# Expert layer of a two-block model: plain fp32 router, first expert pair picked by one-hot products, expert results read back by plain transfers

## The chip, the cores and the metric

The kernel runs on one core of one Trainium2 chip. The metric is the device time of one execution in microseconds, as the median of several runs; lower is better.

## The reference

Two transformer blocks on 512 tokens of 1024 features, all in fp32. The first block (sparse attention, convolution, feed-forward) and the first half of the second (a gated mixer) end in `x`. What the change touches is the second half of the second block, a mixture of 32 experts, and the last norm:

```python
h = modulate(rms_norm_2(x, norm2_g), shift2, scale2)          # (1 + scale2) * norm + shift2
x = x + gate2 * hierarchical_moe(h, ...)
return rms_norm_2(x, final_norm_g)

def hierarchical_moe(h, ...):                                  # 512 tokens, 4 groups of 8 experts
    grp = argmax(softmax(h @ w_group + b_group))               # one group for each token
    top_p, top_e = top_k(softmax((h @ w_router + b_router)[grp]), 2)
    weights = p_grp * top_p / sum(top_p)                       # two experts for each token
    # each token's row goes to its two experts, and the two weighted results are added
    y[token] += (silu(h @ w_gate[e]) * (h @ w_up[e])) @ w_down[e] * weight
```

## The kernel before, in words

The first block fills 0 to about 650 us and the mixer about 650 to 1140 us. From 1140 to 1232 us the output projection of the mixer runs (`join`), with the router beside it; after that the experts run to 1519 us and the last norm to the end.

**Router.** `route_tile` takes a tile of 128 tokens: eight transposes of `x` on PE (L215), their split into two halves of lower precision (ACT L200, DVE L201), the square sum on ACT (L1319) and the inverse root on POOL (`rsqrt`, L211). `rest` makes 24 matmuls with the weights stationary and a transpose back; `end` makes the logits `LT` (L1330), then the normed row `h` (tile `xg`): a multiplication on DVE (L1331) and two additions of 512 columns each (L1334), on POOL for the first three tiles and on DVE for the last. `h` is stored in DRAM (`h2d`, L1335). The four tiles of `h` also stay in the chip's memory as `xg0` to `xg3`.

**Routing.** `route` is a chain of small DVE operations and one-hot products on PE. It gives `tab`, the tokens of each job (`table`, products L1561), and `to`, the place of each result. After the first table, twelve matmuls whose result nobody reads (L1580, `warm`) are on PE. `rest` makes the tables of the other jobs.

**Jobs.** A job (`Pair`) is two experts of up to 64 tokens each; there are 17 (`NP`). The weights are 96 panels of 1 MB, two for each of gate, up and down, loaded by SP into 17 places in rotation (`place`, `panel_of`); a panel starts when the matmuls that read the panel before it in its place are done. Of a job: `gather` (an indirect load by POOL of 128 rows of `h2d`, L1915, into one of two buffers), `turn` (eight transposes, L215, and copies to `xT`, L1928), `up` (64 products of gate and up, L1937, into `a`), `turn_a`, and `down` (16 products, scaled by DVE L1972). Jobs 0 to 12 write rows into `ye` in DRAM (POOL, L1986). Jobs 13 to 16 are "hot" (`HOT` = 13): their rows go back to the tokens on PE, by products with a one-hot matrix `oh` (16 DVE operations, L2000; `spread`, products L2009, additions L2017; the last two jobs in `tail`).

**Results of jobs 0 to 12.** `results` (L1476, L1479) clears a place and gathers for each token the two rows of `ye` that are not hot; for tiles 0 and 1 during job 14, for tiles 2 and 3 during job 15. DVE adds the two rows to `x` one after the other (L1395). A second use of `results`, for experts with more tokens than two jobs hold, is skipped here.

The compiler's scheduler sets the order of the instructions on each engine; POOL's DMAs stand in POOL's order with its arithmetic, and SP's in SP's.

## Time and profile before

| | |
|---|---|
| median of 3 runs | 1540.04 us (1537.99 to 1541.09) |
| the profiled execution's own time | 1541.89 us |
| its span, first to last instruction | 1540.0 us |
| mean granted TensorE clock | 0.978 of full speed |
| PE / DVE / ACT / POOL busy | 95 / 57 / 37 / 13% |
| bytes moved | 266.97 MB, mean 173 GB/s |

The profile is of one execution, and its own time is 1.85 us above the median. Times in its rows count from the first instruction. PE is busy nearly everywhere, so the shares tell little; what counts here is which wait ends last in the stretch from 1224 us to the end.

### The profile page before, as it was taken

To read this page: it belongs to the slowest core of one execution; us is meant where nothing else is said; L and a number is where in the kernel's file an instruction comes from. 1 tells how busy PE (TensorE), PEld (TensorE's weight loads), DVE (VectorE), ACT (ScalarE), POOL (GpSimd) and SP (SyncE) were. 2 spreads that over 40 slices of the span, in tenths; PEclk is the share of its full clock that TensorE was granted. 3 is DMA by queue.
4 is the path that set the end of the run, shared out by engine and by line. 5 is a ranking of instruction groups with operands and counts; after the bars stand their busy time and mean duration, and the time that the engine had idled before them with its cause. 6 is when DMAs were issued, how large, how long until landed. Compare 5 with 4: busy or idle time off the path is not lost.

```text
span 1540.0 us, 20461 instructions
## 1 busy us (share of the span) xinstructions
PE 1460.1 (95%) x7678; PEld 1146.2 (74%) x7678; DVE 883.8 (57%) x1903; ACT 575.5 (37%) x1219; POOL 204.2 (13%) x233
## 2 busy tenths in 40 slices
PE   7999899999999999999999999999999969998885
PEld 6877678787888888887888888888887845555542
DVE  5665687967666764466785452327755763211162
ACT  4444575743242332334444442226643201110112
POOL 2110131100101010040000020000002411111400
PEclk8999999999999999999999999999999979999998
DMA  5225202038665654333322315331149479999971
GB/s 190 91 74 165 93 28 69 28 121 264 199 210 164 203 194 150 124 129 121 96 87 77 84 58 168 130 123 39 45 160 346 164 304 363 420 423 424 423 324 56
DMA packets 132768, 266.97 MB, mean 173 GB/s; under 512 B 19194, under 2 KB 78619, under 8 KB 120376
## 3 DMA queue, kind: packets, MB, share of 16 engines
q1 hardware_dynamic: 119834, 241.90, 43.9%
q0 software_dynamic: 9376, 20.89, 3.7%
q10 hardware_dynamic: 3454, 2.82, 0.6%
q8 instruction: 62, 1.02, 0.3%
q14 instruction: 42, 0.34, 0.1%
HBM read 253.66 MB, written 21.54 MB: 179 GB/s over the span
## 4 chain that ended last, share of the span: by engine, by line
PE 67%; DMA 13%; DVE 6%; ACT 2%; issue 1%; POOL 1%; SPq 0%; ACTq 0%; DVEq 0%; POOLq 0%
PE b L154 18%; PE b L155 18%; PE b L156 18%; PE b L1937 6%; DMA pw<-w_expert_gate 4%; DMA pw<-w_expert_down 3%; PE b L215 3%; DMA pw<-w_expert_up 3%; DMA gm<-gd 1%; DVE wl L148 1%; PE b L819 1%; DMA xg<-h2d,tab 1%; PE b L820 1%; PE b L762 1%; DMA wr<-w_up 1%
## 5 line engine op out<-in xcount | busy, mean ns | idle before, releaser
L148 DVE TENSOR_TENSOR wl<-wr,wh 128x512 fp32r<-128x512 f32 x349 | 237.1, 716 | 146.0 <-ACT wh L146 134.3
L146 ACT ACTIVATE wh<-wr 128x512 fp32r<-128x512 f32 x361 | 205.3, 622 | 301.5 <-PE b L155 142.3
L1937 PE MATMUL b<-pw,xT 128*64 128x256 f32 x1088 | 135.0, 395 | 7.5 <-DMA pw<-w_expert_up 7.1
L1937 PEld LDWEIGHTS b<-pw,xT 128*64 128x64 f32 x1088 | 85.1, 142 | 53.9 <-issue 10.8
L156 PE MATMUL b<-h2h,wl 128*128 128x512 f32 (+1 forms) x320 | 121.3, 379 | 0.0
L154 PE MATMUL b<-h2h,wh 128*128 128x512 f32 (+1 forms) x320 | 121.2, 380 | 0.0
L155 PE MATMUL b<-h2l,wh 128*128 128x512 f32 (+1 forms) x320 | 121.2, 379 | 0.0
L155 PE MATMUL b<-fl,wh 128*128 128x512 f32 (+1 forms) x288 | 105.2, 366 | 0.0
L154 PE MATMUL b<-fh,wh 128*128 128x512 f32 (+1 forms) x288 | 104.9, 366 | 0.3 <-ACT fh L200 0.3
L156 PE MATMUL b<-fh,wl 128*128 128x512 f32 (+1 forms) x288 | 105.1, 366 | 0.0
L155 PE MATMUL b<-wl,uh 128*128 128x512 f32 x256 | 99.9, 390 | 0.5 <-DVE wl L148 0.5
L154 PE MATMUL b<-wh,uh 128*128 128x512 f32 x256 | 100.2, 391 | 0.1
L156 PE MATMUL b<-wh,ul 128*128 128x512 f32 x256 | 99.8, 390 | 0.0
L495 DVE SCALAR_TENSOR_TENSOR acc<-wr,cond,acc 128x512 f32<-128x512 f32 x84 | 62.9, 749 | 38.2 <-DMA wr<-mod_w 36.4
L1954 DVE SCALAR_TENSOR_TENSOR a<-b,ws,a 128x256 f32<-128x256 f32 x17 | 8.2, 483 | 106.5 <-PE b L1937 106.5
L156 PEld LDWEIGHTS b<-h2h,wl 128*128 128x128 f32 x320 | 60.2, 188 | 11.3
L155 PEld LDWEIGHTS b<-h2l,wh 128*128 128x128 f32 x320 | 60.2, 188 | 11.1
L154 PEld LDWEIGHTS b<-h2h,wh 128*128 128x128 f32 x320 | 60.1, 188 | 10.9
L1937 PE MATMUL b<-pw,aT 128*64 128x512 f32 x272 | 64.9, 597 | 0.0
L154 PEld LDWEIGHTS b<-fh,wh 128*128 128x128 f32 x288 | 54.1, 189 | 9.5 <-ACT fh L200 0.5
L155 PEld LDWEIGHTS b<-fl,wh 128*128 128x128 f32 x288 | 54.3, 189 | 9.0 <-DVE fl L201 0.2
L156 PEld LDWEIGHTS b<-fh,wl 128*128 128x128 f32 x288 | 54.3, 189 | 8.8
(601 smaller groups left out, 3256.9 us busy)
## 6 DMA issues: line engine op xcount, KB each, us to landing
wr<-w_in SPq DMA_DIRECT2D x33, 1024.0 KB
pw<-w_expert_gate SPq DMA_DIRECT2D x32, 1024.0 KB
pw<-w_expert_up SPq DMA_DIRECT2D x32, 1024.0 KB
pw<-w_expert_down SPq DMA_DIRECT2D x32, 1024.0 KB
wr<-mod_w SPq DMA_DIRECT2D x24, 1024.0 KB
wr<-w_up SPq DMA_DIRECT2D x16, 1024.0 KB
wr<-w_down SPq DMA_DIRECT2D x16, 1024.0 KB
wr<-w_cmp SPq DMA_DIRECT2D x4, 1024.0 KB
```

The costliest lines, as they stand in the source:

```text
L146: nc.scalar.activation(hi[:, c], raw[:, c], AF.Copy)
L148: (nc.gpsimd if i in pool else eng or nc.vector).tensor_tensor(lo[:, c], raw[:, c], hi.bitcast(F32)[:, c], op=ALU.subtract)
L154: mm(o, lh, rh, start=first, stop=False)
L155: mm(o, lh, rl, start=False, stop=False)
L156: mm(o, ll, rh, start=False, stop=last)
L215: self.nc.tensor.transpose(o, i, self.ident[:k, :k])
L495: nc.vector.scalar_tensor_tensor(acc, rv[:, k, :], self.cond[:, kk:kk + 1], acc, op0=ALU.mult, op1=ALU.add)
L762: nc.tensor.matmul(b[:, :n], QS[:, h, qs], KH[:, kind, g, :n], start=True, stop=False)
L819: nc.tensor.matmul(o, v, ph, start=kind == 2, stop=False)
L820: nc.tensor.matmul(o, v, pl, start=False, stop=kind == 1 and kb == qb)
L1937: self.nc.tensor.matmul(o[h, :], x[:, k, h], w[s](k), start=k == ks[0], stop=k == ks[-1])
L1954: nc.vector.scalar_tensor_tensor(self.a, gu[1], em.ws[:, self.c:self.c + 1], self.a, op0=ALU.mult, op1=ALU.mult)
```

## The change

1. The load of `x` for the mixer of the first block is issued after the fourth step of a plan, in place of before it.
2. The router multiplies in plain fp32: the transposes are copied, one half by ACT and one by DVE, without a split; the tokens are stationary and the 36 columns of weights move, 8 matmuls for a tile in place of 24, and their result needs no transpose.
3. `h` is written with its features in the order (k, p) in place of (p, k), so the operations that write it have a stride of 128 elements; the transposes of a job's rows then read them without a stride.
4. Job 0 isn't gathered. DVE makes a one-hot matrix (`sel`: two multiplications of 128x512 and two additions of 128x256), and `turn` multiplies the four tiles of `h` by it: 32 fp32 matmuls of 128x128. Job 1's rows go to a buffer of their own, and its gather is POOL's first.
5. For jobs 0 to 12, POOL loads all 128x2 rows of `ye` of a tile with one plain transfer (1 MB), adds the two rows itself (128x1024), and DVE adds the sum to `x`.
6. `oh` is made by POOL.

```diff
     def route_tile(self, x, xT, tt):
-            self.split(rh[:, ks, :], rl[:, ks, :], b.rearrange("p (k t) -> p k t", k=4))
+            (nc.vector.tensor_copy if g else nc.scalar.copy)(xT[:, g * 4:g * 4 + 4, :], b.rearrange("p (k t) -> p k t", k=4))
...
             for k in range(KT):
-                self.mm3(lb[:36, ts], wh[:, k, :], wl[:, k, :], rh[:, k, :], rl[:, k, :], k == 0, k == KT - 1)
-            nc.scalar.copy(L, lb[:36, ts])
+                nc.tensor.matmul(lo, xT[:, k, :], w[:, k, :], start=k == 0, stop=k == KT - 1)
...
-            self.transpose(lo, L)
             nc.vector.scalar_tensor_tensor(self.LT[:, tt, :], lo, ss[:, 1:2], bias, op0=ALU.mult, op1=ALU.add)
-            nc.vector.scalar_tensor_tensor(h, xt, ss[:, 1:2], S2, op0=ALU.mult, op1=ALU.mult)
+            pk = lambda a: a.rearrange("t (p k) -> t p k", k=KT)
+            hv = h.rearrange("t (k p) -> t p k", k=KT)
+            nc.vector.scalar_tensor_tensor(hv, pk(xt), ss[:, 1:2], pk(S2), op0=ALU.mult, op1=ALU.mult)
             for g in range(2):
-                s = slice(g * 512, g * 512 + 512)
-                (nc.vector if tt == NT - 1 else nc.gpsimd).tensor_tensor(h[:, s], h[:, s], B2[:, s], op=ALU.add)
+                s = slice(g * 64, g * 64 + 64)
+                (nc.vector if tt == NT - 1 else nc.gpsimd).tensor_tensor(hv[:, s], hv[:, s], pk(B2)[:, s], op=ALU.add)
...
     def moe(self):
-                for j in jobs[:XGS]:
-                    j.gather()
-                nc.gpsimd.dma_start(g2, mod(5).to_broadcast([P, D]))
+                jobs[0].sel = sel
+                jobs[1].gather()
                 jobs[0].turn()
+                nc.gpsimd.dma_start(g2, mod(5).to_broadcast([P, D]))
+                for j in jobs[2:XGS + 1]:
+                    j.gather()
...
                     for tt, y in came:
-                        for k in range(2):
-                            self.pin(nc.vector.tensor_tensor(x[:, tt, :], y[:, k, :], x[:, tt, :], op=ALU.add))
+                        nc.gpsimd.tensor_tensor(y[:, 0, :], y[:, 0, :], y[:, 1, :], op=ALU.add)
+                        self.pin(nc.vector.tensor_tensor(x[:, tt, :], y[:, 0, :], x[:, tt, :], op=ALU.add))
...
-                        self.results(y, src[:, 0], tt)
+                        nc.gpsimd.dma_start(y, self.ye.rearrange("(k t p) d -> t p k d", k=2, t=NT)[tt])
...
     def route(self, ...):
+        for e in range(2):
+            two = oh2[:, :, e * CAP:(e + 1) * CAP]
+            tt_(pick, oc, bc(flat(E)[:, :, e], CAP), ALU.mult)
+            tt_(two, pick[:, 0:4], pick[:, 4:8], ALU.add)
         rows, last = table(vm, SE, slice(0, SE // 2))
...
     def turn(self):
-                em.transpose(b[:, k * P:(k + 1) * P], xv[:, g * 4 + k, :])
+                ks = slice((g * 4 + k) * P, (g * 4 + k + 1) * P)
+                if self.sel is None:
+                    em.transpose(b[:, k * P:(k + 1) * P], self.xg[:, ks])
+                else:
+                    for tt in range(NT):
+                        self.nc.tensor.matmul(b[:, k * P:(k + 1) * P], em.XG[tt][:, ks], self.sel[:, tt, :], start=tt == 0, stop=tt == NT - 1)
...
     def hot(self, kept):
-            nc.vector.tensor_scalar(self.oh[:, tt * P:(tt + 1) * P], em.rt[3], kept[:, self.c:self.c + 1], -float(tt * P), op0=ALU.subtract, op1=ALU.is_equal)
+            nc.gpsimd.tensor_scalar(self.oh[:, tt * P:(tt + 1) * P], em.rt[3], kept[:, self.c:self.c + 1], -float(tt * P), op0=ALU.subtract, op1=ALU.is_equal)
```

How the scheduler orders the changed program shows at three places. PE between the routing and job 0, in the changed kernel; the four tiles `xg` are the normed rows, `S` holds `sel`, and the row with `xg` alone is job 1's transposes:

```order
L1566 MATMUL b_10791<-q_10780,oc 64x6 x8
L1590 MATMUL b_10806<-oc 128x512 x12
L1937 MATMUL b_10836<-S_10015,xg_10028 128x128
L1937 MATMUL b_10836<-S_10015,xg_10029 128x128
...
L1937 MATMUL b_10854<-S_10015,xg_10030 128x128
L1937 MATMUL b_10854<-S_10015,xg_10031 128x128
L215 MATMUL b_10981<-ident,xg 128x128 x4
L1947 MATMUL b_10993<-pw_10433,xT_10835 64x256
L215 MATMUL b_10987<-ident,xg 128x128 x4
L1947 MATMUL b_10993<-pw_10435,xT_10835 64x256
```

Where two rows of transposes of job 0's gathered rows stood, 32 products now stand; job 1's transposes still stand ahead of all but one of job 0's products.

POOL at the end of the job loop, first before and then in the changed kernel (`pw` is a place, `o` a job's result):

```order
L1986 DMA ye<-o_12239,to 1024x1024
L1476 MEMSET pw_12333 128x2048
L1476 MEMSET pw_12334 128x2048
L1479 DMA pw_12333<-ye,src 128x1024 x2
L1479 DMA pw_12334<-ye,src 128x1024 x2
L1476 MEMSET pw_12488 128x2048
L1476 MEMSET pw_12489 128x2048
L1479 DMA pw_12488<-ye,src 128x1024 x2
L1479 DMA pw_12489<-ye,src 128x1024 x2
```

```order
L1996 DMA ye<-o_12180,to 1024x1024
L1400 DMA pw_12274<-ye 128x2x1024
L1400 DMA pw_12275<-ye 128x2x1024
L1393 TENSOR_TENSOR pw_12274<-pw_12274 128x1024
L1393 TENSOR_TENSOR pw_12275<-pw_12275 128x1024
L2010 TENSOR_SCALAR oh_12456<-rt,kept 128x128 x4
L1400 DMA pw_12417<-ye 128x2x1024
L1400 DMA pw_12418<-ye 128x2x1024
L1393 TENSOR_TENSOR pw_12417<-pw_12417 128x1024
L1393 TENSOR_TENSOR pw_12418<-pw_12418 128x1024
```

The loads of tiles 2 and 3 now stand behind two additions that need the loads of tiles 0 and 1, and behind job 15's `oh`, whose buffer was job 13's.

DVE and PE where job 14 is spread, in the changed kernel (`x` additions L2027 of `spread`, L1394 of the read results; on PE the products L2019 of `spread`, L1947 of job 16's gate):

```order
L2027 TENSOR_TENSOR x_10012<-b_12506,x_10012 128x512
L1964 SCALAR_TENSOR_TENSOR a_12414<-b_12381,ws,a_12414 128x256
L1982 TENSOR_TENSOR o_12454<-b_12461,S_10015 128x512
L1982 TENSOR_TENSOR o_12454<-b_12469,S_10015 128x512
L1394 TENSOR_TENSOR x_10012<-pw_12417,x_10012 128x1024
L201 TENSOR_TENSOR pw_12455<-o_12454,pw_12455 128x512
L1394 TENSOR_TENSOR x_10012<-pw_12418,x_10012 128x1024
L201 TENSOR_TENSOR pw_12455<-o_12454,pw_12455 128x512
L2027 TENSOR_TENSOR x_10012<-b_12514,x_10012 128x512
```

```order
L1947 MATMUL b_12495<-pw_12483,xT_12307 64x256
L2019 MATMUL b_12531<-k_12422,oh_12424 128x512
L2019 MATMUL b_12531<-k_12423,oh_12424 128x512
L1947 MATMUL b_12495<-pw_12485,xT_12307 64x256
L1947 MATMUL b_12495<-pw_12483,xT_12307 64x256
L1947 MATMUL b_12495<-pw_12485,xT_12307 64x256
```

The two read additions L1394 took the place of four; the third addition of spread 14 (`b_12514`) stands behind both, and on PE the fifth product of spread 14 (`b_12531`), which waits for it, stands behind one of job 16's sixteen gate rows, with fifteen behind it; before, all sixteen stood ahead of it.

## Rows read from the trace of the kernel before

**Rows 1.** The page: share of the DMA engines in 40 slices of 38.5 us, in tenths.
```profile
DMA  5225202038665654333322315331149479999971
```

**Rows 2.** Stretches: busy us of each engine, mean granted clock, DMA share, GB/s.
```profile
1254.00:1258.00 4.00, 2.99 (x10) 1.86 (x10) 1.16 (x6) 0.58 (x1) 0.92 (x1) 0.50 0.77 317
...
1260.00:1266.00 6.00, 6.00 (x39) 3.47 (x39) 4.96 (x19) 1.66 (x3) 0.00 (x0) 0.67 0.00 0
...
1284.00:1490.00 206.00, 191.25 (x1295) 109.93 (x1297) 49.73 (x78) 22.19 (x48) 40.85 (x37) 0.98 1.01 421
```

**Rows 3.** Timeline of SP's queue, 1230 to 1300: start, us, line, tile.
```profile
1282.61 0.33 SPq L1718 DMA_DIRECT2D pw<-w_expert_gate  x1
```

**Rows 4.** PE waits in total, 1284 to 1450: us, times, longest.
```profile
PE b L1937 <- DMA pw<-w_expert_up: 7.1, 4, 2.8
```

**Rows 5.** Timeline of PE, 1224 to 1300: start, us, line, count, [idle before].
```profile
1227.04 1.04 PE L215 MATMUL b<-ident,x 128*128 128x128 f32 x8
...
1244.42 5.47 PE L1580 MATMUL b<-oc 128*128 128x512 f32 x12
...
1254.86 1.95 PE L215 MATMUL b<-ident,xg 128*128 128x128 f32 x8 [4.97 <-DMA xg<-h2d,tab]
...
1260.38 6.72 PE L1937 MATMUL b<-pw,xT 128*64 128x256 f32 x44
...
1284.60 7.13 PE L1937 MATMUL b<-pw,xT 128*64 128x256 f32 x64
```

**Rows 6.** Timeline of DVE, 1228 to 1285.
```profile
1229.86 1.29 DVE L1334 TENSOR_TENSOR xg<-xg,B 128x512 f32<-128x512 f32 x2
...
1236.29 0.26 DVE L1330 SCALAR_TENSOR_TENSOR LT<-b,ss,rb 128x36 f32<-128x36 f32 x1 [0.41 <-PE b L215]
...
1243.07 0.76 DVE L1509 TENSOR_TENSOR oc<-rt,q 128x256 fp32r<-128x256 f32 x2
```

**Rows 7.** Groups of DVE by form: busy us, mean ns; L791 contiguous, L1527 with a stride.
```profile
L791 DVE TENSOR_REDUCE cst<-cs 128x4 f32<-128x128 f32 x8 | 2.2, 278 | 0.1
...
L1527 DVE TENSOR_REDUCE q<-q 128x32 f32<-128x128 f32 x1 | 0.4, 374 | 0.0
```

**Rows 8.** Groups of POOL by form: busy us, mean ns of one.
```profile
L1334 POOL TENSOR_TENSOR xg<-xg,B 128x512 f32<-128x512 f32 x6 | 8.6, 1450 | 4.2 <-DVE xg L1331 4.2
...
L777 POOL TENSOR_SCALAR p<-p,st 128x128 f32<-128x128 f32 x4 | 2.4, 608 | 12.5 <-DVE st L775 5.2 <-DVE st L769 3.5 <-PE b L156 3.5
```

**Rows 9.** Timeline of PE, 911.5 to 916: an fp32 product is two records.
```profile
912.24 0.38 PE L1161 MATMUL b<-dg,ones 128*128 128x128 f32 x2
912.46 0.60 PE L215 MATMUL b<-ident,hl 128*128 128x128 f32 x4
```

**Rows 10.** Timeline of POOL, 1430 to 1540: the first and the last read of results.
```profile
1449.55 1.02 POOL L1479 DMA_INDIRECT pw<-ye,src  x1 [5.46 <-DMA ye<-o,to]
...
1462.53 0.99 POOL L1479 DMA_INDIRECT pw<-ye,src  x1 [0.30 <-issue]
```

**Rows 11.** DMA issues by form: count, KB each, median us from issue to landing.
```profile
S<-modrow POOLq DMA_DIRECT2D x1, 512.0 KB, 9.3
...
pw<-ye,src POOLq DMA_INDIRECT x8, 14.4
```

**Rows 12.** Queues, 1436 to 1475: packets, MB, share of the engines; q0 is POOL's.
```profile
q0 software_dynamic: 1189, 2.90, 18.7%
```

**Rows 13.** Timeline of DVE, 1455 to 1520.
```profile
1471.79 1.21 DVE L1395 TENSOR_TENSOR x<-pw,x 128x1024 f32<-128x1024 f32 x1
```

**Rows 14.** Timeline of PE, 1436 to 1530.
```profile
1471.93 0.73 PE L2009 MATMUL b<-k,oh 128*128 128x512 f32 x2 [0.86 <-DVE x L2017]
...
1475.83 3.67 PE L1937 MATMUL b<-pw,xT 128*64 128x256 f32 x32
...
1497.82 1.33 PE L2009 MATMUL b<-k,oh 128*128 128x512 f32 x4 [1.90 <-DVE x L2017]
...
1500.87 3.67 PE L1937 MATMUL b<-pw,xT 128*64 128x256 f32 x30
```

More of the change, by code (lines that the diff above doesn't have):

```diff
@@ L367, in block1 @@
             x1 = self.xp.tile([P, NT, D], F32, tag="x", name="x1")
-            for tt in range(NT):
-                nc.sync.dma_start(x1[:, tt, :], I["x"][0, tiles[tt], :])
             with ExitStack() as c2:
@@ L374, in block1 @@
                 done = []
-                for step in PLAN:
+                for i, step in enumerate(PLAN):
+                    if i == 4:
+                        for tt in range(NT):
+                            nc.sync.dma_start(x1[:, tt, :], I["x"][0, tiles[tt], :])
                     r = next({"u": att, "c": conv, "m": mix}[step])
@@ L1232, in join @@
                         self.split(gh[:, j, :], gl[:, j, :], ga, 0.5)
-                self.logits = (self.bank("l"), self.bank("l"))
+                self.logits = self.bank("l")
                 later = []
@@ L1248, in join @@
                                 if i < NT:
-                                    later.append(self.route_tile(x, yp.tile([P, 2, KT, P], F32R, tag="al", name=self.nm("rhl"), bufs=2), i))
+                                    later.append(self.route_tile(x, yp.tile([P, KT, P], F32, tag="al", name=self.nm("rx"), bufs=2), i))
                                 else:
@@ L1288, in prepare @@
             wide = lambda a: a.unsqueeze(2).to_broadcast([P, 8, 36])
-            sw, bw = (gb[:, i * 288:(i + 1) * 288].rearrange("p (k c) -> p k c", k=8) for i in range(2))
-            nc.vector.tensor_tensor(sw, raw, wide(cols[:, 0:8]), op=ALU.mult)
+            bw = gb[:, 0:288].rearrange("p (k c) -> p k c", k=8)
+            nc.vector.tensor_tensor(wx, raw, wide(cols[:, 0:8]), op=ALU.mult)
             nc.vector.tensor_tensor(bw, raw, wide(cols[:, 8:16]), op=ALU.mult)
-            self.split(wh, wl, sw)
             nc.vector.tensor_reduce(bs, bw.rearrange("p k c -> p c k"), axis=AX.X, op=ALU.add)
@@ L1348, in moe @@
             self.eid = rp.tile([P, ND], I32, tag="eid", name="eid")
-            src = rp.tile([P, 2, 8], I32, tag="src", name="src")
+            src = rp.tile([P, 8], I32, tag="src", name="src")
             self.xi = rp.tile([P, NX], I32, tag="xi", name="xi")
@@ L1357, in moe @@
             with self.pool("r1", 1) as r1:
-                rest = self.route(r1, rp, tab, to, src, W, xb, sc, kept, ws)
+                sel, rest = self.route(r1, rp, tab, to, src, W, xb, sc, kept, ws)
             self.banks(t="y", u="z", c="w", d="x")
@@ L1361, in moe @@
                 ep = c1.enter_context(self.pool("ep", 1))
-                XG = list(self.XG)
-                jobs = [Pair(self, ep, XG[i % XGS], tab, to, i) for i in range(NP)]
+                early = ep.tile([P, D], F32, tag="o", name="xg", bufs=2)
+                jobs = [Pair(self, ep, early if i == 1 else self.XG[i % XGS], tab, to, i) for i in range(NP)]
                 n = len(jobs)
-                for j in jobs[:XGS]:
-                    j.gather()
-                nc.gpsimd.dma_start(g2, mod(5).to_broadcast([P, D]))
+                jobs[0].sel = sel
+                jobs[1].gather()
                 jobs[0].panels = self.early + [self.panel_of(*w) for w in PANELS(0)[EARLY:]]
                 jobs[0].turn()
-                rest(*(ep.tile([P, D], F32, tag="o", name="rq", bufs=2) for _ in range(2)))
+                nc.gpsimd.dma_start(g2, mod(5).to_broadcast([P, D]))
+                for j in jobs[2:XGS + 1]:
+                    j.gather()
+                rest([ep.tile([P, T], F32, tag="oh", name="rq", bufs=2) for _ in range(2)], ep.tile([P, D], F32, tag="o", name="rq", bufs=2))
                 gf = self.xp.tile([P, D], F32, tag="B2", name="gf")
@@ L1379, in moe @@
                         jobs[i + 1].turn()
-                    if i + XGS < n:
+                    if 0 < i and i + XGS < n:
                         jobs[i + XGS].gather()
@@ L1421, in moe @@
                         y = self.wr.tile([P, 2, D], F32, tag="wr", name=self.nm("y"))
-                        self.results(y, src[:, 1], tt)
+                        self.results(y, src, tt)
                         for k in range(2):
@@ L1583, in route, with rest @@
             V.tensor_copy(cum, b[:, 0:160])
-        def rest(room, room2):
-            tl, tl2 = carve(room), carve(room2)
+        def rest(rooms, room2):
+            tl, tl2 = carve(*rooms), carve(room2)
             cnt = cum[:, 128:160]
@@ L1693, in rest @@
             V.tensor_scalar(self.xi, xe, ip, None, op0=ALU.add)
-        return rest
+        return oh2, rest
     def place(self, dt=F32):
@@ L1908, in __init__ @@
         self.nc = em.nc
-        self.panels = None
+        self.panels = self.sel = None
     def tl(self, tag, *shape, bufs=2, dt=F32):
```

34 lines of the change are left out of this document (16 added, 18 removed).

## The prediction, made before the changed kernel ran

> **What bounds the kernel now.** I read the DMA slices first [rows 1]: the DMA engines are far from full until the experts, and full for nearly all of them. The stretches say it sharper [rows 2]: from 1284 to 1490 us the share is 1.01 at 421 GB/s, while in 1260 to 1266 nothing moves at all. The gap has one cause, found in SP's queue [rows 3]: all 17 places hold panels that wait for their readers, and the load at 1282.61 us starts when job 0's down products, the last readers of its panels, are done. So the stretch before is bound by the start of job 0, and the time lost there is lost to the whole stream behind it. That the stream then sets the pace shows in PE's waits from 1284 to 1450 [rows 4]: four for an up panel, 7.1 us in all. Whatever the release of job 0's panels gains, I take to pass 1:1 as far as there. After 1450 no wait of PE for a panel is left; the end is PE and DVE in turn, and the results of jobs 0 to 12 have to be in `x` before the hot additions go on.
>
> What holds job 0 stands in PE's timeline [rows 5]. The twelve unread products end at 1249.89. Then PE is idle 4.97 us until the first gather has landed; job 0's transposes start at 1254.86, and the products in earnest at 1260.38. The clock there is at 1.2 GHz: 0.50 granted in 1254 to 1258 after those idle microseconds [rows 2]. 44 products took 6.72 us, against 64 in 7.13 later at full clock [rows 5].
>
> **The change, part by part.**
>
> *The moved load of `x`, the split of the router weights, the fewer copies.* 0: SP's order is unchanged, and the others stand beside the 95% busy PE in a stretch where the output projection's products set the pace. If that cover were gone, some 2 us of DVE work would be saved at most.
>
> *Router.* Before, the logits of the last tile are done at 1236.55 [rows 6]. The new order on PE needs, from 1224.7, three more groups of transposes (1.04 each [rows 5]) and 4x16 records of fp32 products; at 0.11 to 0.13 each (half of the 0.22 us that two records took [rows 9]; a transpose's 1.04/8) these are 7.0 to 8.3, so PE alone gives 1234.9 to 1236.1. But `h` is now written with a stride, and the last tile's copy stands on DVE behind the normed row of that tile, which waits for POOL, which first finishes its two additions of tile 2 (1.45 each [rows 8]). Against the contiguous row of the same 128 elements the strided one took 0.374 for 0.278 us, 35% more [rows 7]. On the chain of two multiplications on DVE (1.3 each), POOL's pair (2.9) and DVE's pair (1.3 [rows 6]), 6.8 us, that is up to 2.4. The upper end is then 1237.8. I take 1236.2, a gain of 0.3, and keep -1.6 to +1.3.
>
> POOL's two strided additions are where a page speaks against the change. The Trainium skill, GPSIMD Engine Reference, section "Performance pitfalls for Q7 kernels", gives about 2.9 in place of 1.9 cycles an element for reads with a step of over 8 bytes, half as much again. By it POOL's pair would take about 4.4 us, half a microsecond above the 35%, and the sum would be 0.5 later; no row before has POOL with a stride.
>
> *Pick in place of gather 0.* Removed: the gather, its wait of 4.97 and its transposes. Added on DVE: two multiplications and two additions ahead of the first table, about 1.1 us later for `tab`; the wait for gather 1 then ends near 1255, under the pick's cover. Added on PE: 32 fp32 products, 64 records. At 0.129 they take 8.3 us; the bounds are 7.0 (64 x 0.11 [rows 9]) and 14.1, at 0.22 a record, as if the records ran at 1.2 GHz or every load of weights stood open. I take 8.3, since the unread products run right ahead of them without a gap, and the clock rose within 1260 to 1266 before (0.67 in the mean of that stretch [rows 2]) after less work than that. So: logits 1236.2, plus 7.3 to the end of the one-hot columns (1236.55 to 1243.83 [rows 6]), plus 0.9 for the table, plus 5.5 for the unread products, plus 8.3, is 1258.2. Job 1's transposes (1.0) then fill the copy to `xT`, and products start at 1259.3 at full clock: 1.1 earlier, and 44 of them cost 1.8 less (6.72 - 44 x 0.111). Job 0's panels come free 2.9 us earlier, **-3**. Ends: -5.5 (records at 0.11, router at 1234.9) and +4 (pick 14.1, router 1237.8).
>
> Behind the new waits: gate2's row and gathers 2 and 3 stand on POOL behind the pick (`S` and the buffers are its operands). Gate2 is first used by job 0's scaling near 1279, 20 us later, against 9.3 from issue to landing [rows 11]: 0. Contiguous transposes are worth about 0.3 us a job and lie in the stage that waits for panels: 0.
>
> *Results and `oh`.* Before, reads are issued from 1449.55 to 1463.5 [rows 10] and land with a median of 14.4 [rows 11]. Queue q0 moved 2.90 MB in 1436 to 1475 [rows 12], about 1.0 of it a gather and a write of jobs, so the reads were about 1.9 MB; now all rows are 4.2 MB. The additional 2.3 MB cost 5.5 us of a full stream (421 GB/s): PE's panels had room by then (no wait after 1450), so 0 there. But the reads themselves come late. Tiles 0 and 1, 2.1 MB from 1449.6: the lower bound is 14.4 as before, the upper 37 (four times 9.3 for 512 KB [rows 11], one after another). I take 22, near the gathers. POOL's sum of tile 1 (2 x 1.45 [rows 8]) ends at about 1475, DVE's addition at 1476; before, the last of these ended at 1473.0 [rows 13]. PE's products of spread 13, at 1471.93 to 1475.8 before [rows 14], end 1475 to 1481. Only then may POOL make job 15's `oh` (4 x 0.61 [rows 8] = 2.4), and only then issue tiles 2 and 3: 1478 to 1484, where it was 1458 to 1463. With 14 to landing, 2.9 for the last sum and 1.2 for the addition, DVE is through at 1496 to 1502; I take 1500.5 for the fifth product of spread 14. Before, it ran at 1497.82 [rows 14], with all of job 16's gate products done. Now 15 of these 16 rows, 30 records, stand behind it: 3.4 us (30 in 3.67 [rows 14], less the overlap). The new order is even at 1494.4; at 1500.5 it loses 6.1, and PE after such an idle time runs at the lower clock for a while, as at 1254 [rows 2], about 1: **+7**. Ends: -2 (four fewer additions of 1.22 [rows 13], if every read is in time) and +11 (the reads at the upper pace).
>
> **Sum.** 1541.9 - 3 + 7 = 1546 by the profiled execution, which ran 1.85 above the median: **1544**.
>
> **The rivals.**
>
> *The reads come in time.* For it: the additions of tile 2 and 3 had room until 1490 before, since they stand behind job 15's scaling, and the panel stream ends near 1490, which frees the engines. Against it: issue behind spread 13 and `oh`. It decides at 1494.4. Then the tail is -2 to 0 and the front -3 to -5.5: 1541.9 - 4 - 1 - 1.85 = **1535**, faster.
>
> *The pick runs slow.* At 0.22 us a record the pick takes 14.1 us: front +2.5 with the tail's +7, **1549.5**. It decides at 11.2 us for the pick. For it: the clock was 0.50 before and the unread products took 0.46 us each, twice what 512 columns take elsewhere; against it: two fp32 records with weights of their own took 0.22 together at full clock [rows 9]. The Trainium skill, TensorE: Matmul & The Clock Gate, section "The mechanism", says that a load of weights overlaps running products only where their row groups differ, which would hold every one of these 64 loads open; by it the sum would be this rival's. By that rule, [rows 9] could not be: two records with their loads and the next transpose stand 0.22 apart.
>
> *Job 0 is not freed.* Job 1's transposes stand ahead of all but one of job 0's products. If gather 1 lands later than the pick ends, the change has moved the wait and not taken it away: front -1 to 0, tail +7, **1546.5**. Against it: job 1's gather is issued first now, and it has the pick's 8 us more to land.
>
> *Front and tail cancel*: tail +3 by faster reads, front -3: **1540**.
>
> **How the numbers follow.** The forecast has 0.35, reads in time 0.27, slow pick 0.12, not freed 0.10, cancelling 0.16. About 0.2% is what a measurement of this kernel can tell from none: 1537 to 1543. The forecast's own range, 1541 to 1549, lies mostly above: 0.25 of its 0.35. Faster takes 0.26 of the reads in time and 0.03 of cancelling, 0.29; same the other 0.13 of cancelling, 0.09 of the forecast and 0.03 of the rest, 0.25; slower what is left, 0.46. The range takes 1533 (front -5.5, tail -2) to 1551 (slow pick with the tail's +7 and some of the upper end); the likeliest case alone is 1541 to 1549.
>
> **What would show it.** Right: 64 records of L1937 after the unread products, some 8 us long, directly followed by job 1's transposes; the SP load that stood at 1282.61 at about 1280; POOL issuing tiles 2 and 3 after 1478 with PE waiting for DVE before the fifth product of spread 14, and the gate products of job 16 behind it. Wrong: a pick of over 11 us; PE idle ahead of job 1's transposes; PE without a wait of over 2 us between 1470 and 1505, which would mean that the reads come in time; or a front gain that is gone by 1440 since panels set the pace by another place than job 0's.

## The result, and the profile after

The changed kernel took **1550.11 us** (median of 8 runs, 1546.74 to 1558.12) beside 1540.57 us for the kernel before (8 runs, 1537.99 to 1544.42): a ratio of 1.0069, 95% interval 1.0046 to 1.0092, so 7 to 14 us more (9.5 by the medians) where +4 was forecast. The profiled execution took 1548.82 us, its span is 1547.0 us, and its mean granted clock 0.978, as before.

In the profiled pair the front went as forecast. PE's timeline of the changed kernel around the start of the experts (start, us, line, count, [idle before]; to set beside [rows 5]; L1322 is the router, L1590 the unread products, L1937 the pick, L1947 the jobs' products):

```profile
1230.77 1.95 PE L1322 MATMUL b<-rwx,rx 128*128 128x36 f32 x16 [1.22 <-DVE LT L1325]
...
1240.98 5.47 PE L1590 MATMUL b<-oc 128*128 128x512 f32 x12
1246.25 7.65 PE L1937 MATMUL b<-S,xg 128*128 128x128 f32 x64
1254.12 0.63 PE L215 MATMUL b<-ident,xg 128*128 128x128 f32 x4 [0.21 <-DMA xg<-h2d,tab]
...
1255.84 1.95 PE L1947 MATMUL b<-pw,xT 128*64 128x256 f32 x16
```

The wait of 4.97 us for the first gather is gone, 0.21 is left for job 1's, and the pick's 64 records took 7.65 us (0.12 each). The stretches, to set beside [rows 2] (busy us of each engine, granted clock, DMA share, GB/s):

```profile
1254.00:1258.00 4.00, 3.88 (x31) 2.38 (x31) 3.29 (x10) 1.87 (x2) 1.61 (x2) 1.00 0.44 162
1260.00:1266.00 6.00, 5.96 (x53) 4.17 (x49) 4.86 (x12) 0.76 (x2) 5.45 (x7) 1.00 0.75 253
...
1284.00:1490.00 206.00, 184.89 (x1248) 104.49 (x1244) 47.68 (x74) 22.58 (x48) 37.58 (x34) 0.99 1.00 418
1490.00:1500.00 10.00, 0.61 (x2) 0.50 (x2) 4.80 (x6) 0.00 (x0) 2.34 (x1) 0.64 0.12 48
```

The clock at 1254 to 1258 is 2.4 GHz (1.00) where it was 1.2 (0.50). The last row is the loss: ten microseconds near the end in which PE worked 0.61 us, the DMA engines were nearly idle, and the clock fell to 0.64 in the mean.

SP's load that waits for job 0's panels ([rows 3]: 1282.61):

```profile
1276.36 0.33 SPq L1724 DMA_DIRECT2D pw<-w_expert_gate  x1
```

It is 6.25 us earlier. But 3.38 of that was there before the router's end: its bias product (L1295) ran at 1198.40 for 1201.78, and this start lies anywhere from 1196 to 1210 in the kernels below. From the last logits (1233.18) it is 43.18 us, where it was 46.06 (1282.61 - 1236.55).

POOL near the end (L1400 loads results, L1393 sums two rows, L2010 makes `oh`):

```profile
1443.13 1.50 POOL L1400 DMA_DIRECT2D pw<-ye  x2 [8.56 <-DMA ye<-o,to]
1454.93 2.35 POOL L1393 TENSOR_TENSOR pw<-pw 128x1024 f32<-128x1024 f32 x1 [10.30 <-DMA pw<-ye]
1462.01 3.10 POOL L1393 TENSOR_TENSOR pw<-pw 128x1024 f32<-128x1024 f32 x1 [4.73 <-DMA pw<-ye]
1472.41 3.64 POOL L2010 TENSOR_SCALAR oh<-rt,kept 128x128 fp32r<-128x128 f32 x4 [7.29 <-PE b L2019]
1476.00 1.52 POOL L1400 DMA_DIRECT2D pw<-ye  x2
1487.58 2.34 POOL L1393 TENSOR_TENSOR pw<-pw 128x1024 f32<-128x1024 f32 x1 [10.05 <-DMA pw<-ye]
1494.54 2.34 POOL L1393 TENSOR_TENSOR pw<-pw 128x1024 f32<-128x1024 f32 x1 [4.63 <-DMA pw<-ye]
```

The second pair of loads starts at 1476.00, behind 7.29 us of waiting for spread 13 and behind `oh`; before, the reads of these tiles were issued by 1463.5 [rows 10]. Tile 2 can be summed 11.6 us after the issue, tile 3 18.5 us after it. The four loads together (count, KB each, median us from issue to landing) have much the median that the prediction took:

```profile
pw<-ye POOLq DMA_DIRECT2D x4, 1024.0 KB, 14.7
```

But DVE needs the last of the pair. DVE and PE behind it (L1394 adds tile 3's sum, L2027 is the addition of spread 14; on PE L2019 is the fifth product of spread 14; [rows 13, 14]):

```profile
1496.91 1.23 DVE L1394 TENSOR_TENSOR x<-pw,x 128x1024 f32<-128x1024 f32 x1 [5.14 <-POOL pw L1393]
1498.05 0.69 DVE L201 TENSOR_TENSOR pw<-o,pw 128x512 fp32r<-128x512 f32 x1
1498.66 1.28 DVE L2027 TENSOR_TENSOR x<-b,x 128x512 f32<-128x512 f32 x2
```

```profile
1443.23 3.70 PE L1947 MATMUL b<-pw,aT 128*64 128x512 f32 x16
...
1487.41 0.59 PE L1947 MATMUL b<-pw,xT 128*64 128x256 f32 x2
1499.39 1.22 PE L2019 MATMUL b<-k,oh 128*128 128x512 f32 x2 [11.38 <-DVE x L2027]
1500.55 4.84 PE L1947 MATMUL b<-pw,xT 128*64 128x256 f32 x32
```

PE waits 11.38 us with one gate row of job 16 done (two records) and the others behind. Between the two places the panel stream sets the pace as before (PE's waits from 1284 to 1450, [rows 4]: 7.1):

```profile
PE b L1947 <- DMA pw<-w_expert_up: 7.6, 4, 2.8
```

**Stage by stage.** Since the start of the experts differs by more than the effect, I compare stages, not spans: differences of starts of rows in each profile, in us. The columns: the router's bias product to the last logits; the last logits to the SP load that needs job 0's panels; from there to the first down product of job 13 (1443.23 above, 1449.03 before); from there to the first root of the last norm on POOL (L230), the tail; and the tail's two parts, up to the fifth product of spread 14 and from it on. What each kernel is stands with the experiments.

| kernel | router | to the release | to job 13 | tail | up to the fifth product | from it on |
|---|---|---|---|---|---|---|
| before | 34.77 | 46.06 | 166.42 | 73.34 | 48.79 | 24.55 |
| the change | 34.78 | 43.18 | 166.87 | 86.00 | 56.16 | 29.84 |
| e1 moved load alone | 34.76 | 44.15 | 168.70 | 74.81 | 48.71 | 26.10 |
| e12 router alone | 36.29 | 45.61 | 167.44 | 74.88 | 48.70 | 26.18 |
| e2 router and pick alone | 34.77 | 43.99 | 166.74 | 73.67 | 49.12 | 24.55 |
| e3 results and `oh` alone | 34.76 | 45.67 | 166.59 | 86.71 | 56.38 | 30.33 |
| e4 change, `oh` by DVE | 36.41 | 43.34 | 168.71 | 76.56 | 46.79 | 29.77 |
| e5 change, `oh` and sums by DVE | 34.77 | 43.35 | 166.83 | 76.33 | 51.87 | 24.46 |
| e6 change, sums by DVE | 36.44 | 42.90 | 166.86 | 84.31 | 57.63 | 26.68 |
| e7 change, gate rows first | 35.85 | 42.90 | 167.23 | 81.98 | 55.43 | 26.55 |
| e8 change, `oh` by DVE, gate rows first | 34.76 | 43.88 | 166.78 | 72.82 | 48.33 | 24.49 |
| e9 change, late loads by SP | 34.77 | 43.09 | 166.92 | 82.53 | 48.47 | 34.06 |

In the profiled pair the stages add up: -2.9, +0.4 and +12.7, less the 3.4 of the earlier start, are 6.8, and the two profiled executions differ by 6.9 us. How far one profile's tail can be trusted shows in e1 and e12, whose tails have the code of the kernel before and are 1.5 longer: the wait before the fifth product is 1.90 in all three, but behind it the clock fell in e1 (0.65 in 1498 to 1502) and did not in the kernel before (1.00). The profiled executions of e3 and e7 ran 7.7 and 8.9 us above their medians; both reached the router late, at 1209.67 and 1208.86.

### The profile page after: what moved, and what is told of

It reads as the page before. It is cut to its first block, busy times and chain, and to the rows that moved or that the text cites. A ratio compares the mean times of both kernels' runs of the same rounds, so it can differ in the third digit from the quotient of the medians.

```text
span 1547.0 us, 20474 instructions
## 1 busy us (share of the span) xinstructions
PE 1463.3 (95%) x7698; PEld 1152.0 (74%) x7698; DVE 879.8 (57%) x1879; ACT 572.6 (37%) x1210; POOL 216.3 (14%) x244
## 3 DMA queue, kind: packets, MB, share of 16 engines
q8 instruction: 63, 1.03, 0.3%
## 4 chain that ended last, share of the span: by engine, by line
PE 63%; DMA 9%; issue 8%; DVE 7%; POOL 2%; ACT 2%; POOLq 0%; ACTq 0%; DVEq 0%
PE b L155 18%; PE b L156 18%; PE b L154 18%; DMA ye<-o,to 4%; DMA pw<-ye 2%; PE b L215 2%; PE b L1947 1%; DVE wl L148 1%; PE b L821 1%; PE b L2019 1%; DMA xg<-h2d,tab 1%; PE b L822 1%; PE b L764 1%; DMA wr<-w_up 1%; PE b L765 1%
## 5 line engine op out<-in xcount | busy, mean ns | idle before, releaser
L1947 PE MATMUL b<-pw,xT 128*64 128x256 f32 x1088 | 132.1, 387 | 9.9 <-DMA pw<-w_expert_up 8.3
L1947 PEld LDWEIGHTS b<-pw,xT 128*64 128x64 f32 x1088 | 85.2, 139 | 54.9 <-DMA pw<-w_expert_up 10.8
L156 PEld LDWEIGHTS b<-h2h,wl 128*128 128x128 f32 x320 | 60.6, 189 | 11.4
L1947 PE MATMUL b<-pw,aT 128*64 128x512 f32 x272 | 66.1, 597 | 0.5 <-ACT aT L1973 0.5
```

The lines of the kernel that those rows point to most:

```text
L156: mm(o, ll, rh, start=False, stop=last)
L1947: self.nc.tensor.matmul(o[h, :], x[:, k, h], w[s](k), start=k == ks[0], stop=k == ks[-1])
```

## The experiments

Ratios are times over those of the kernel before in runs on the same chip, with 95% intervals; as recorded, they can differ by 0.1% from the quotient of the two medians. e1 to e4 shared a chip (before: 1541.61 us), so did e5 to e8 (1541.34) and e9 to e12 (1541.84).

**e1: the moved load alone** (part 1 on the kernel before).

```diff
-            for tt in range(NT):
-                nc.sync.dma_start(x1[:, tt, :], I["x"][0, tiles[tt], :])
...
-                for step in PLAN:
+                for i, step in enumerate(PLAN):
+                    if i == 4:
+                        for tt in range(NT):
+                            nc.sync.dma_start(x1[:, tt, :], I["x"][0, tiles[tt], :])
```

> The kernel before with part 1 of the change alone (the load of x for the first block's mixer issued after the fourth step of the plan). In the changed kernel's profile the first block is 4.3 us shorter, and the wait of DVE at 160 us for the constants k_dist and k_cbias (three transfers of ACT's queue, issued beside that load) is 3.6 in place of 6.4 us. Theory A, the moved load does it: 1536 us, and the wait for the constants near 3.6 us. Theory B, the instructions stand in the same order on every engine, so the 4.3 us are what executions differ by: 1540.5 us, 0 within 0.2%.

Measured: 1542.27 us, ratio 1.0003 (0.9980 to 1.0027). DVE's timeline, first before, then e1, at its wait for a table of constants:

```profile
163.56 0.69 DVE L766 CUSTOM_DVE_ANT_0 p<-b,base 128x512 f32<-128x512 f32 x1 [6.42 <-DMA base<-k_dist]
```

```profile
160.81 0.69 DVE L768 CUSTOM_DVE_ANT_0 p<-b,base 128x512 f32<-128x512 f32 x1 [3.67 <-DMA base<-k_dist]
```

The move does something there: the wait is 2.75 us shorter (3.23 to 3.67 in all twelve profiles with the moved load, 6.42 and 6.66 in the two without), and at 650 us a step of the second block (L228) stands at 650.21 for 654.52. By 1201 the two are level (1201.35 and 1201.78). So the move is real and no gain of it shows in the time, whose interval would hide one of up to 3 us.

**e12: the router alone** (parts 1 to 3), with job 0 gathered and the results read as before.

```diff
-                jobs[0].sel = sel
+                jobs[0].gather()
                 jobs[1].gather()
```

(The operations that make `sel` are left out as well, and parts 5 and 6 undone.)

> The changed kernel without the pick (job 0 gathered, its gather first on POOL) and with the results read and oh made as before: the fp32 router and the order of the features alone. From the end of the router's bias product to the last logits 34.8 us as before, or 36.4 where a copy comes late; from the last logits to the release of job 0's panels 44 to 46 us as in the three profiles without the pick, against 42.9 to 44.0 with it. Theory A (the router is worth nothing, all that the front gains is the pick's): 1540 to 1542 us. Theory B (the contiguous transposes or the router gain by themselves): 1538 us or less.

Measured: 1542.18 us, ratio 0.9994 (0.9970 to 1.0018); the release is 45.61 after the logits, within what the three other kernels that gather job 0 have (44.15 to 46.06). The router is worth nothing that can be measured.

**e2: router and pick alone** (parts 1 to 4; parts 5 and 6 undone).

> Parts 1 to 4 of the change, with the results of jobs 0 to 12 read as before (cleared places, gathers, two DVE additions) and the one-hot matrix oh made by DVE as before. Theory A (the front gains what was forecast, and all of the loss lies in the reading of the results): job 0's down products end 3 us earlier counted from the start of the router, and the time is 1537.5 us without, 1534 us with a gain of the moved load. Theory B (a part of the loss is in the router or the pick, or the front's gain is used up by the panels before 1440): 1540 us or more.

Measured: 1540.51 us, ratio 1.0000 (0.9981 to 1.0019). The pick took 7.41 us, and the release stands 43.99 after the logits. So the pick does what it should, but the forecast's -3 doesn't show in the time; the interval leaves room for a gain of up to 2.9 us.

**e3: results and `oh` alone** (parts 5 and 6 on the kernel before).

```diff
-                        for k in range(2):
-                            self.pin(nc.vector.tensor_tensor(x[:, tt, :], y[:, k, :], x[:, tt, :], op=ALU.add))
+                        nc.gpsimd.tensor_tensor(y[:, 0, :], y[:, 0, :], y[:, 1, :], op=ALU.add)
+                        self.pin(nc.vector.tensor_tensor(x[:, tt, :], y[:, 0, :], x[:, tt, :], op=ALU.add))
...
-                        self.results(y, src[:, 0], tt)
+                        nc.gpsimd.dma_start(y, self.ye.rearrange("(k t p) d -> t p k d", k=2, t=NT)[tt])
...
-            nc.vector.tensor_scalar(self.oh[...
+            nc.gpsimd.tensor_scalar(self.oh[...
```

> The kernel before with parts 5 and 6 alone (plain transfers of the results, their sum on POOL, oh on POOL). Theory A (the loss lies here, 13 us by the two profiles): 1553 us, with a wait of PE of about 11 us before the fifth product of spread 14. Theory B (the loss comes of the results meeting a stream that the earlier front has shifted): 1545 us or less, a wait under 6 us.

Measured: 1555.44 us (6 runs), ratio 1.0082 (1.0058 to 1.0106), as theory A had it. The wait stands in e3's timelines of POOL and PE (lines 2009 and 1937 are the change's 2019 and 1947):

```profile
1489.71 1.52 POOL L1401 DMA_DIRECT2D pw<-ye  x2
...
1508.22 2.34 POOL L1394 TENSOR_TENSOR pw<-pw 128x1024 f32<-128x1024 f32 x1 [4.45 <-DMA pw<-ye]
```

```profile
1513.07 1.22 PE L2009 MATMUL b<-k,oh 128*128 128x512 f32 x2 [10.99 <-DVE x L2017]
1514.22 5.29 PE L1937 MATMUL b<-pw,xT 128*64 128x256 f32 x32
```

The whole loss comes with these two parts: a tail of 86.71, a wait of 10.99, and again 18.5 us from the issue to the sum of tile 3.

**e4: the change with `oh` made by DVE**, so that POOL's second pair of loads doesn't stand behind it.

```diff
-            nc.gpsimd.tensor_scalar(self.oh[:, tt * P:(tt + 1) * P], em.rt[3], ...
+            nc.vector.tensor_scalar(self.oh[:, tt * P:(tt + 1) * P], em.rt[3], ...
```

> The changed kernel with oh made by DVE as before, so on POOL the loads of tiles 2 and 3 stand right behind the sum of tile 1 and no longer behind the wait for spread 13. Theory A (the place in POOL's order is the cause): these loads are issued near 1465 in place of 1476 us, land before 1487, the wait of 11.4 us goes, 1534 to 1538 us. Theory B (the additional bytes of the plain transfers, 4.2 for 1.9 MB, are the cause, wherever they are issued): 1546 us or more.

Measured: 1546.15 us, ratio 1.0030 (1.0013 to 1.0047). POOL and PE of e4:

```profile
1466.62 1.46 POOL L1400 DMA_DIRECT2D pw<-ye  x2
...
1486.18 2.34 POOL L1393 TENSOR_TENSOR pw<-pw 128x1024 f32<-128x1024 f32 x1 [4.13 <-DMA pw<-ye]
```

```profile
1496.67 1.22 PE L2019 MATMUL b<-k,oh 128*128 128x512 f32 x2 [4.48 <-DVE x L2027]
1497.82 4.77 PE L1947 MATMUL b<-pw,xT 128*64 128x256 f32 x32
```

The loads go as soon as POOL's sums are done, and DVE no longer waits for them: the sum of tile 3 is done at 1488.5, but DVE adds it behind job 15's scaling. Yet some 5 us are still lost, and the time stands at theory B's bound of 1546. But the bytes are not the reason (e5 has the same bytes and not the loss): the fifth product stands 46.79 us after job 13's first down product, 2.0 earlier than before the change, and the loss lies behind it (29.77 for 24.55). PE stands 4.48 us where it could have multiplied: the gate rows of job 16 still stand behind the fifth product.

**e5: plain loads only**: the change with `oh` and both sums by DVE. The scheduler then puts the gate rows first.

> The changed kernel with oh made by DVE and both additions of the results on DVE as before; of parts 5 and 6 only the plain transfers are left, all four in a row on POOL. On PE all sixteen gate rows of job 16 stand ahead of the fifth product of spread 14 again. Theory A (place and order are the cause, the bytes cost nothing): 1538 to 1542 us, like the kernel with router and pick alone, the wait before the fifth product under 2.5 us. Theory B (4.2 for 1.9 MB crowd the panels or land too late): 1545 us or more.

Measured: 1539.61 us, ratio 0.9993 (0.9971 to 1.0014). PE of e5:

```profile
1459.60 5.35 PE L1947 MATMUL b<-pw,xT 128*64 128x256 f32 x30 [2.32 <-DMA pw<-w_expert_up]
...
1493.22 4.10 PE L1947 MATMUL b<-pw,xT 128*64 128x256 f32 x34
...
1498.09 1.33 PE L2019 MATMUL b<-k,oh 128*128 128x512 f32 x4 [0.77 <-DVE x L2027]
```

The additional bytes of the plain loads cost nothing that shows in the time: the second pair is issued from 1450.17 on, long before it is needed. In this profile the tail is 3.0 longer than before: PE waited 2.32 us for an up panel, and the 30 records behind it ran at the lower clock (0.66 in 1460 to 1465), 5.35 us for 3.67. That is not the price of the bytes by itself: e8, with plain loads too, has the same wait (2.33) with the clock up behind it (1.00 in 1456 to 1460), and a tail of 72.82.

There are also fewer of these bytes than the 2.3 MB of the prediction. POOL's queue over the whole execution, in the kernel before and in e3 (packets, MB, share of the engines):

```profile
q0 software_dynamic: 9376, 20.89, 3.7%
...
q0 software_dynamic: 9312, 22.03, 3.9%
```

They are 1.1 MB. The window of [rows 12] ends at 1475, when the indirect reads were not all done: 0.66 MB of this queue moved in 1475 to 1482, so the reads were about 3.0 MB and not 1.9.

**e6: the change with the sums by DVE**, `oh` still by POOL.

> The changed kernel with the two additions of the results on DVE as before, oh still on POOL: the loads of tiles 2 and 3 still stand behind oh of job 15 and so behind spread 13, but nothing waits on POOL for a sum, and on PE all gate rows of job 16 stand ahead of the fifth product of spread 14. Theory A (the place behind spread 13 makes the late landing, the order on PE a part of the price): loads issued 1474 to 1478 us, landed near 1494, the fifth product near 1500, 1545 to 1548 us, some 4 less than the changed kernel. Theory B (POOL's sums are the cause, 2.3 to 3.1 us each): 1541 us or less.

Measured: 1550.15 us (6 runs), ratio 1.0063 (1.0041 to 1.0086). POOL and PE of e6:

```profile
1478.60 3.76 POOL L2010 TENSOR_SCALAR oh<-rt,kept 128x128 fp32r<-128x128 f32 x4 [34.42 <-PE b L2019]
1482.31 1.49 POOL L1400 DMA_DIRECT2D pw<-ye  x2
```

```profile
1489.71 4.10 PE L1947 MATMUL b<-pw,xT 128*64 128x256 f32 x34
...
1502.98 2.08 PE L2019 MATMUL b<-k,oh 128*128 128x512 f32 x4 [9.17 <-DVE x L2027]
```

POOL idles for 34.42 us and still issues the loads at 1482.31: the place behind `oh`, which waits for spread 13, is the cause, and not POOL's sums. The 4 us that theory A took off the changed kernel's time did not come: the issue stands 37.0 us after job 13's first down product, for 32.8 in the changed kernel, since `oh` came later still. Here the gate rows stood ahead (34 records at 1489.71) and the wait was 9.17 all the same, so the order on PE alone isn't the cure.

**e7: the change with the gate rows first**: the later half of spread 14 is held on PE until the last gate row of job 16. **e8: the same with `oh` by DVE.**

```diff
...
+            if self.c == NP - 1 and i == 0:
+                em.gate = self.last
...
-            self.onto(b, tt, half, True, True)
+            if half and self.c == NP - 3:
+                with self.em.tc.issue_after(self.em.gate.ins):
+                    self.onto(b, tt, half, True, True)
+            else:
+                self.onto(b, tt, half, True, True)
```

(`last` is the matmul issued last by the job, here the last gate row of job 16.)

> The changed kernel with one edit: the last four steps of spread 14 are held on PE until the last gate row of job 16 is issued, so that 15 rows (30 records, 4.8 us in the changed kernel's profile at the lower clock) fill the wait of 11.4 us. Theory A (these rows behind the wait are a term of their own): 1545 to 1547 us, 4 to 5 less than the changed kernel, the wait 7 us. Theory B (the end is set by the reads alone and the rows find room elsewhere): within 1.5 us of the changed kernel.

> The changed kernel with both edits: oh on DVE and the gate rows of job 16 ahead of the fifth product of spread 14; POOL keeps the plain loads and the sums, DVE four additions fewer than before. Theory A (the two edits take away all of the loss): 1536 to 1539 us, below the kernel before, the wait under 2 us. Theory B (something else of the results costs as well): 1542 us or more.

Measured, e7: 1547.56 us, ratio 1.0042 (1.0024 to 1.0060), tail 81.98 for 86.00. e8: 1540.25 us, ratio 0.9999 (0.9980 to 1.0019), tail 72.82. PE of e7, then of e8 (L2021 and L2033 are the change's L2019 and L2027):

```profile
1498.05 4.05 PE L1947 MATMUL b<-pw,xT 128*64 128x256 f32 x34
...
1510.27 2.07 PE L2021 MATMUL b<-k,oh 128*128 128x512 f32 x4 [8.17 <-DVE x L2033]
```

```profile
1485.10 4.05 PE L1947 MATMUL b<-pw,xT 128*64 128x256 f32 x34
...
1490.17 1.32 PE L2021 MATMUL b<-k,oh 128*128 128x512 f32 x4 [1.03 <-DVE x L2033]
```

In e7 the wait shrinks by 3.2 us, since the gate rows fill it, and the tail by 4.0; in e8, with the loads early too, all of the loss is gone. With e4 this splits it: the loads' lateness is worth some 9 us of the tail (86.0 to 76.6, or 82.0 to 72.8), the order of the gate rows some 4 (86.0 to 82.0, or 76.6 to 72.8). By time it is some 6 us for the lateness (ratios 1.0069 to 1.0030, or 1.0042 to 0.9999) and some 4.5 for the order (1.0069 to 1.0042, or 1.0030 to 0.9999), each known to about 4 us. Job 16's `oh`, which e4 and e8 take off POOL too, was not waited for in the changed kernel: it was done at 1510.81, and PE was at job 16's rows until 1512.21.

**e9: the change with tiles 2 and 3 loaded by SP**, so that no arithmetic of POOL stands ahead of the loads.

```diff
-                        nc.gpsimd.dma_start(y, self.ye.rearrange(...
+                        (nc.sync if tt >= 2 else nc.gpsimd).dma_start(y, self.ye.rearrange(...
```

> The changed kernel with the loads of tiles 2 and 3 issued by SP in place of POOL (oh and sums stay on POOL). Theory A (the wait is made by the place behind spread 13 and by POOL's own queue, which lands the second MB of a pair 18.5 us after issue even after the panels have ended): issued before 1476 us, landed by 1487, a wait of PE of 5 us or less in place of 11.4, 1541 to 1545 us. Theory B (the landing is as slow on any queue, the memory or the 16 engines set it): 18 us to landing here too, 1547 us or more.

Measured: 1545.91 us, ratio 1.0031 (1.0016 to 1.0046). This lies between the two theories. SP issued the loads from 1458.64 on; POOL's sums stand behind `oh`, which is done at 1475.98. SP, POOL and PE of e9:

```profile
1458.64 3.96 SPq L1400 DMA_DIRECT2D pw<-ye  x2
```

```profile
1479.44 2.35 POOL L1393 TENSOR_TENSOR pw<-pw 128x1024 f32<-128x1024 f32 x1 [3.47 <-DMA pw<-w_expert_up]
1482.06 2.35 POOL L1393 TENSOR_TENSOR pw<-pw 128x1024 f32<-128x1024 f32 x1 [0.27 <-DMA pw<-w_expert_down]
```

```profile
1491.60 0.72 PE L2019 MATMUL b<-k,oh 128*128 128x512 f32 x2 [4.03 <-DVE x L2027]
...
1493.33 2.08 PE L2019 MATMUL b<-k,oh 128*128 128x512 f32 x4 [1.01 <-DVE x L2027]
```

POOL still waited 3.47 us for SP's queue before the sum of tile 2. The profile names an up panel of that queue, so whether the loads themselves or the panels issued behind them ended the wait isn't shown, nor whether SP's queue lands such a pair sooner: the sum starts 20.8 us after the issue. By time some half of the loss goes; by the tail (82.53) it is 3.5 of 12.7 us. The fifth product stands where it stood before the change (48.47 for 48.79), but the scheduler has put all sixteen gate rows of job 16 behind it, and from there to the end it is 34.06 for 24.55. So e9 tests the early issue together with a worse order on PE.

**e10: e8 with job 1's transposes behind job 0's products**; **e11: e10 without the twelve unread products** (L1590 left out; their result is used nowhere).

```diff
-                    if i + 1 < n:
+                    if 0 < i and i + 1 < n:
                         jobs[i + 1].turn()
...
+                    if i == 0:
+                        with self.tc.issue_after(j.last.ins):
+                            jobs[1].turn()
```

> The kernel with oh on DVE and the gate rows first, and job 1's transposes held on PE until job 0's gate and up products are issued. Theory A (the rival of the prediction: the pick's gain is cut by gather 1, for which job 1's transposes wait ahead of job 0's products, 0.2 to 1.0 us, and their own 1.3 us): job 0's products follow the pick directly, 1.5 to 2.5 us earlier, and the time is 0.1 to 0.2% under the kernel with oh on DVE and gate rows first. Theory B: no difference, since the restart of the panels hangs on job 0's down products, ahead of which job 1's transposes stand anyway.

> The same without the twelve unread products. Theory A (they keep the pick at the upper clock): the pick starts 5.3 us earlier but runs at the lower clock, 13 to 14 us in place of 7.5, and job 0's products start within 1 us of where they did: same time within 0.2%. Theory B (the clock rises within the pick): job 0's products start 3 us earlier and the time is 0.2% lower.

Measured, e10: 1537.35 us, ratio 0.9974 (0.9958 to 0.9990), the only kernel here that is below the one before by more than its interval. Job 0's products follow the pick directly, 20.4 us after the logits for 22.7 in the changed kernel (1255.84), as theory A had it. But its release is 43.0 after the logits, within what the others with a pick have, as theory B had it, so where its 4 us come from isn't shown, and its interval overlaps that of e8. e11: 1539.31 us, ratio 0.9991 (0.9973 to 1.0009). PE of e11 and its stretches:

```profile
1245.68 8.81 PE L1938 MATMUL b<-S,xg 128*128 128x128 f32 x64 [2.03 <-DVE tab L1516]
```

```profile
1244.00:1248.00 4.00, 2.32 (x11) 2.35 (x12) 3.94 (x23) 0.21 (x1) 1.14 (x1) 0.50 1.01 428
1248.00:1252.00 4.00, 4.00 (x35) 4.00 (x35) 4.00 (x34) 1.23 (x3) 0.00 (x0) 0.91 1.00 421
```

Without the unread products the pick starts at 1.2 GHz and the clock rises within it: 8.81 us for 7.43 in e10. Neither theory came out: the pick is far under A's 13 to 14 us, and job 0's products start 1.7 us earlier where B had 3. The release is 1.7 us earlier too (41.29 after the logits), and the time isn't better: another sign that one or two microseconds at the release can't be told in the end.

## Why the prediction was right or wrong

The direction, the place and the mechanism were right: the loads wait behind `oh`, PE waits before the fifth product, and gate rows stand behind it. The size was off by more than the forecast itself, +9.5 for +4. That the range held the time is largely luck: its upper end, 1551, was made for a slow pick, which did not come, and the tail's loss of 12.7 lies outside the -2 to +11 that the prediction kept for it.

- **The failing step** is the landing in the tail's term: "With 14 to landing, 2.9 for the last sum and 1.2 for the addition, DVE is through at 1496 to 1502; I take 1500.5 for the fifth product of spread 14." In us after job 13's first down product (1449.03 in the trace of before) that said an issue at 29 to 35 and a fifth product at 51.5. Measured: the issue at 32.8 (1476.00 - 1443.23), the fifth product at 56.16. The issue was right, in part by luck: tile 1 could be summed 18.9 us after the first pair's issue and not 22, and `oh` took 3.64 us and not 2.4. The 14 was the median over indirect reads [rows 11]. The plain loads have much the same median, 14.7, but what ends the wait is the last of the pair, at 18.5. That alone is +4.5. The sum (2.34) and the addition (1.23) were about as priced. A longer time was at hand: the first pair was priced at 22, and for less in the second the prediction has only the thought that the panel stream ends near 1490 and frees the engines. The first pair could be used after 11.8 and 18.9 us with the engines full, the second after 11.6 and 18.5 while the panels ended.
- **The gate rows behind the fifth product** were priced at 3.4 and the lower clock at 1. From the fifth product to the end of the stage it is now 29.84 us (86.00 - 56.16) for 24.55 before (73.34 - 48.79): 5.3 for 4.4. The table tells the two apart: with the gate rows ahead of a long wait (e6, e7) this part is 26.7 and 26.6, so the clock cost some 2.1 and the place of the rows some 3.2; the rows were priced well and the clock at half. The rows right after the wait took 4.84 us for 32 records, where [rows 14] has 3.67 for 30. Together with the wait (56.16 for 48.79, 7.4) the tail lost 12.7 where 7 was forecast.
- **The front, -3.** In the profiled pair it came out to the digit, 0.0 for the router and -2.9 from the logits to the release, but one pair's agreement is luck. Over the profiles it is smaller: 45.4 (44.15 to 46.06) in the mean of the four kernels that gather job 0 and 43.3 (42.90 to 43.99) in the eight of the table that pick it, so -2.0; and the router came out at +0.7 in the mean where I took -0.3, since in four of nine it took over a microsecond longer, up to 1.7, outside the +1.3 that I had kept (in e4 the last group of its products, after a wait of 1.22 for DVE, took 3.57 us for the 1.95 above, with 0.50 granted in 1234 to 1238). About -1.3 is left, which e2 by time neither shows nor excludes.
- **Sum.** -1.3 + 12.7 = 11.4, within the measured 7 to 14.
- **The strided `h`.** DVE's multiplication, of which only the result has a stride, rose from 1.28 to 2.04 us in the mean, 59%, and its additions from 0.69 to 1.03, 50%: more than the 35% of [rows 7], whose two reductions also differ in what they write (4 and 32 results). POOL's additions of the same shape rose from 1.45 to 1.79, 24%. The rule weighed in the prediction (the Trainium skill, GPSIMD Engine Reference, "Performance pitfalls for Q7 kernels": half as much again, stated for kernels written for that engine) is more than POOL showed.
- **The rivals.** "The reads come in time" fell: the wait is 11.38. "The pick runs slow" fell: 0.12 us a record. The weight loads were busy beside the products (3.90 and 4.00 of 4 us in 1246 to 1250), so they stand under them, against the rule as the prediction read it (the Trainium skill, TensorE: Matmul & The Clock Gate, "The mechanism"). The same section says, which the prediction did not weigh, that a load for the background weight buffer is also pulled ahead of running products, and with that the trace agrees. "Job 0 is not freed" fell: a wait of 0.21. "Cancel" fell on the tail, not on the front.
- **What I costed at nothing.** The moved load and the additional bytes, 1.1 MB and not 2.3, show nothing by time (e1, e5). That PE has no wait for a panel after 1450 no longer holds: behind job 13 it waited once more for an up panel, 0.71 us in the changed kernel and 2.1 to 2.3 in e5 to e8, but also 0.87 in e12 without the new loads, so the loads aren't shown to be the cause.

## What to carry to other kernels

A DMA issued by an engine that also computes stands in that engine's order: here the move of `oh`, four small operations for each job, to POOL put two loads behind a wait for PE (issued at 1476.00, right behind `oh`; with `oh` on DVE, right behind the sum), and cost some 6 us, where the rest of the change gained nothing that shows by time. Price a pair of transfers by the landing of the last one, not by a median, and when a wait is added, look which independent work stands behind it on the waiting engine; moving either the loads or that work ahead takes a part back (e4, e7), both take back all (e8). Where one stretch starts up to 13 us apart from execution to execution, compare stages from a common mark, and trust a gain of 1 to 2 us at an early stage only if the time shows it.

## What the runs showed of the hardware that I had not expected

- A pair of plain 1 MB loads by POOL could be used after 11.8 and 18.9 us while panels filled the engines (share 1.02 in 1443 to 1462), and after 11.6 and 18.5 when the panels ended on the way (0.84 in 1482 to 1488, 0.27 in 1488 to 1495). In e6, with the pair issued at 1482.31 and the share at 0.55 in 1488 to 1494, it was 11.6 and 16.5. So freer engines took at most some 2 us off the last load, and nothing off the first.
- A stride of 128 elements cost the engines differently on the same addition of 128x512: 24% on POOL, 50% on DVE.
- POOL took 2.8 to 3.64 us for the four operations of `oh`, DVE 0.87 (e5).
- The clock rose within the pick itself in e11, from 0.50 in 1244 to 1248 to 0.91 in the mean of 1248 to 1252. In that profile the products that nobody reads would have saved 1.4 us of the pick, and leaving them out let it start 3.1 us earlier after the logits.
